# A parallel-branch decoder layer on one core: the work behind each z pair dealt out one step per product, a pair's last product one place later, and SSD groups at equal distances

## The chip, the cores and the metric

The kernel runs on one core of one Trainium2 chip. The metric is device time in microseconds (us) of one execution. The engines are TensorE (PE; its weight loads are listed as PEld), VectorE (DVE), ScalarE (ACT), GpSimd (POOL) and SyncE (SP). Each takes its instructions in the order in which the program lists them. SP issues most loads, POOL most stores, and ACT a few loads.

## The reference

One layer with x of 1024 tokens by 1024 channels in float32:

```
xn   = rms_norm(x)
proj = xn @ w_in                       # za, zb, zc, xbc, dt, gates: 10256 columns
ya   = gmlp(za)                        # chunked spatial gating, 8 groups
yb   = gelu(gate) * rg_lru(conv(xb))   # 8 heads of 128 channels
y    = ssd(conv(xbc), dt)              # 4 groups of 256 channels, chunks of 128 tokens
yc   = group_rms_norm(y * silu(zc)) * norm_g        # each group of 256 channels by itself
h    = x + (sum over a,b,c of sigmoid(g_k) * (y_k @ w_branch_k)) @ w_out
out  = rms_norm(h + relu(rms_norm(h) @ w_up)^2 @ w_down)
```

The line that this case turns on is yc: `z` is one of the projections, and after it is known there is a tanh (for the silu), two multiplications, a square, a sum over 256 channels, a reciprocal root and one more multiplication.

## The kernel before, in words

All large products are made of float32 operands split in a high and a low part (`split`, L128 to L133: ACT writes the high part, DVE subtracts it for the low part), with three matmuls for each block (high by high, high by low, low by high).

The program has five stages, in this order of the span: the normalised input and the first v blocks; the *first stage proper* (units of one weight column of 128, by `one_unit`, L558: 48 matmuls of 128x512 each and then a `post` function on the result); the *pair stage*; the merge of the three branches and w_out; and the MLP.

**Units (L1025 to L1045).** Four SSD groups, each with four units (b, c, x0, x1), stand in the queue with LRU heads between them: after group 0 the heads 0 and 1, after group 1 the heads 2 and 3, after group 2 the head 4 alone, after group 3 the heads 5, 6 and 7 (6 and 7 have a second unit each for the gate). Eight gMLP units follow. When the last unit of a group is posted, a generator (`ssd_stages`, L644) is put on the list `pending`. `step()` (L539) takes every pending generator one `yield` further, and runs once per unit. An SSD group's generator has eight such parts: broadcast rows of the decay are loaded, then transposes, products and the decay (`s1_`), the states (`s2_`), the outputs (`s3_`), and the same for the other half of the tokens. `s1_` and `s3_` take PSUM tiles `aux`, of which there are four in all: `s3_` takes four of them (two each for `yo` and `yi`). In this stage a scheduler sets the final order of instructions on each engine.

**Pairs (L901 to L1013).** The gates of the three branches (kind "t"), the z projection of the SSD branch ("z") and six of the eight LRU gate columns ("g") are not units but pairs of columns, and each pair is a 256-wide product done by a seven-product scheme on halves (`seventh`, L473: 12 matmuls of 128x512). The products are called p1, p2, p5, p6, p3, p7, p4 in their order. p1, p6, p7 and p4 add into one PSUM tile, `b1` (of the pool `gps`, four tiles); p5 and p3 into `b2` (an `aux` tile); p2 uses a `gps` tile of its own. So a product that adds into a tile waits until the engine that read it last has done so:

- after p1 ACT copies b1 (L971); p6 adds into b1 next
- after p2 DVE adds its tile to the copy (L976)
- after p5 ACT copies b2 (L982); p3 adds into b2 next
- after p6 ACT copies b1 (L988); p7 adds into b1 next
- after p3 DVE adds (L992), after p7 DVE adds (L996); p4 adds into b1 next
- after p4 ACT copies or gates (L915, L917)

There are 19 pairs, in the order t z t g t, t z t g t, t z t g t, z t t t. The loop that runs them is L1269 to L1311, with the order of the program kept as written. During a pair the weights of the next one are prepared: `cast1`, `cast12`, `cast34`, `cast22` are splits (one ACT and one DVE instruction each), `sums1` and `sums2` are four DVE additions (L502 to L507). p4 of the pair before (`prev.p4()`) stands behind p1 of the present pair. `step()` runs after each product, seven times per pair.

**Behind a z pair.** When a half (512 tokens) of a z pair is complete, `post_z` (L943 to L965) becomes pending: half 1 after p7, half 0 after p4. Its parts before the change, one per step: (A and B) tanh on ACT, two DVE multiplications of 128x1024, square on ACT; (C) a DVE addition of 128x512 (L950); an empty step; then all of (E to I): a matmul with a matrix of ones (L954), a root on ACT (L956, with a table load before it), a reciprocal on DVE (L957), four short DVE instructions (L958 to L961), two DVE multiplications (L964) and the store of the result on POOL's queue (L965). `post_g` (L933) does the like for a g pair in two parts: square, a DVE instruction and tanh; then two DVE multiplications and the store. The tiles `x` that they use come from a pool of four (`actx`).

Of the kernel before, what the change touches and what calls it, by code (L numbers as in the profile page):

```python
# [36 lines left out]
def trunk_kernel(ctx: ExitStack, tc: tile.TileContext, x, norm_mix_g, w_in, b_gate, gmlp_ln_g, gmlp_ln_b,  # L37
# [30 lines left out]
    def nm(s):  # L68
        uid[0] += 1
        return f"{s}_{uid[0]}"  # L70
# [7 lines left out]
    def aux():  # L78
        return auxp.tile([P, HF], F32, tag="aux", name=nm("aux"))
# [459 lines left out]
    def step():  # L539
        for g_ in list(pending):  # L540
            try:
                next(g_)
            except StopIteration:
                pending.remove(g_)
# [79 lines left out]
    def ssd_units(g):  # L624
        S = {}

        def xbc(key, ct):
            def post(ps):
                c = act()
                conv(c, ps, [scw[:, j * 16 + ct:j * 16 + ct + 1] for j in range(4)], vh[:, SCB + ct:SCB + ct + 1])  # L630
                t = act()
                actv(t, c, AF.Tanh)
                stt(out=c, in0=t, scalar=1.0, in1=c, op0=ALU.add, op1=ALU.mult)
                S[key] = c
                if key == "x1":
                    later(ssd_stages(g, S))
            unit_in(C_XBC + ct * P, post)

        xbc("b", 8 + g)
        xbc("c", 12 + g)  # L640
        xbc("x0", 2 * g)
        xbc("x1", 2 * g + 1)
# [109 lines left out]
    def lru_units(h):  # L752
# [60 lines left out]
        if h >= PLAIN:  # L813
            unit_in(C_GATE + h * P, post_g)
# [83 lines left out]
    def actx():  # L898
        return actx_pool[0].tile(list(two), F32, tag="actx", name=nm("x"))

    class Pair:  # L901
# [31 lines left out]
        def post_g(self, half):  # L933
            o, y, t = self.o[half], self.y[half], actx()
            actv(t, o, AF.Square)
            stt(out=t, in0=t, scalar=1.0 / GELU_C, in1=o, op0=ALU.add, op1=ALU.mult)
            actv(t, t, AF.Tanh, scale=GELU_S * GELU_C)
            yield
            stt(out=o, in0=t, scalar=1.0, in1=o, op0=ALU.add, op1=ALU.mult)
            tt(out=o, in0=o, in1=y, op=ALU.mult)  # L940
            nc.gpsimd.dma_start(out=self.part(yd["b"], half), in_=o)

        def post_z(self, half):  # L943
            o, y, t = self.o[half], self.y[half], actx()
            actv(t, o, AF.Tanh, scale=0.5)
            stt(out=o, in0=t, scalar=1.0, in1=o, op0=ALU.add, op1=ALU.mult)
            tt(out=o, in0=o, in1=y, op=ALU.mult)
            actv(t, o, AF.Square)
            yield
            tt(out=t[:, 0], in0=t[:, 0], in1=t[:, 1], op=ALU.add)  # L950
            yield
            yield
            vs = aux()
            mm(vs, ones, t[:, 0], start=True, stop=True)  # L954
            r, q = y[:, 0], y[:, 1]
            actv(r, vs, AF.Sqrt, scale=1.0 / 256, bias=eps4)  # L956
            nc.vector.reciprocal(out=r, in_=r)  # L957
            tt(out=q, in0=r, in1=r, op=ALU.mult)  # L958
            stt(out=q, in0=vs, scalar=256 * 4.0 * EPS, in1=q, op0=ALU.add, op1=ALU.mult)
            ts(out=q, in0=q, scalar1=-0.5 / 256, scalar2=1.5, op0=ALU.mult, op1=ALU.add)  # L960
            tt(out=r, in0=r, in1=q, op=ALU.mult)  # L961
            for b in range(2):
                col = SNG + self.e + b
                stt(out=o[:, b], in0=o[:, b], scalar=va[:, col:col + 1], in1=r, op0=ALU.mult, op1=ALU.mult)  # L964
            nc.gpsimd.dma_start(out=self.part(yd["c"], half), in_=o)  # L965
# [56 lines left out]
        yield  # L1022
        z.w.cast12()

    for r, heads in enumerate(((0, 1), (2, 3), (4,), (5, 6, 7))):  # L1025
        ssd_units(r)
        for h in heads:
            lru_units(h)
# [52 lines left out]
    def w_load(b, name, new, key=None):  # L1081
        L[b, key or name] = [new(two) for _ in range(2)]
        for h, t in enumerate(L[b, key or name]):
            nc.sync.dma_start(out=t, in_=w_view(b, name, h))
# [7 lines left out]
    def y_first(b, new):  # L1092
        R[b, "first"] = [new(two, F32R) for _ in range(2)]
        for h, t in enumerate(R[b, "first"]):
            nc.sync.dma_start(out=t.bitcast(F32), in_=y_view(b, "B21", h))
# [10 lines left out]
    def sums_load(b):  # L1106
        w_load(b, "A21", w4, "S")
        for h in range(2):
            add_into(L[b, "S"][h], w_view(b, "A22", h))
# [10 lines left out]
    def make(b, i, s):  # L1120

        side, h = (s // 2) ^ (i == 3), s % 2
        new = op_new(b, i, side)
        pr = OP.setdefault((b, i), ([], []))[side]
        if side == 0:
            src = L[b, ("A12", "A11", "S", "A12", "S", "A21", "A22")[i]][h]
            hi, lo = new(two, F32R), new(two, F32R)
            split(hi, lo, src)
            if i == 2:
                actv(src, src, AF.Copy, scale=-1.0)  # L1130
                add_into(src, L[b, "A11"][h])
                for k in range(2 * h):
                    add_into(L[b, "A12"][k], L[b, "S"][k])
            elif i == 4:
                t = L[b, "A21"][h]
                tt(out=t, in0=L[b, "A11"][h], in1=t, op=sub)
        elif i == 0:
            lo = R[b, "first"][h]
            hi = new(two, F32R)
            split(hi, lo, lo.bitcast(F32))  # L1140
        else:
            hi, lo = new(two, F32R), new(two, F32R)
            split(hi, lo, R[b, ("", "B11", "B11", "B22", "B11", "B12", "B21")[i]][h])
            r = lambda name: R[b, name][h]
            if i == 1:
                tt(out=r("B11"), in0=r("B12"), in1=r("B11"), op=sub)
            elif i == 3:
                tt(out=r("B11"), in0=r("B11"), in1=r("B22"), op=sub)
                tt(out=r("B12"), in0=r("B22"), in1=r("B12"), op=sub)
            elif i == 4:  # L1150
                tt(out=r("B21"), in0=r("B21"), in1=r("B11"), op=ALU.add)
        pr.append((hi, lo))
# [115 lines left out]
    z, prev = cur.pop(), None  # L1268
    with tc.manual_schedule():  # L1269
        z.w.cast22()  # L1270
        while z:
            nxt = Pair(*pairs.pop(0)) if pairs else None
            z.p1()
            z.w.cast34()
            step()
            if prev:
                prev.p4()
                step()
            z.p2()
            if nxt:  # L1280
                nxt.w.cast1()
            else:
                w_load(0, "A12", r4)
                y_first(0, act)
                w_load(0, "A11", w4)
            step()
            z.p5()
            if nxt:
                nxt.w.sums1()
            else:  # L1290
                make(0, 0, 2)
            step()
            z.p6()
            if nxt:
                nxt.w.sums2()
                nxt.w.cast12()
            else:
                sums_load(0)
                make(0, 0, 3)
            step()  # L1300
            z.p3()
            if nxt:
                nxt.w.cast22()
            else:
                make(0, 0, 0)
            step()
            z.p7()
            if not nxt:
                make(0, 0, 1)
            step()  # L1310
            prev, z = z, nxt  # L1311
# [312 lines left out]
    with tc.manual_schedule():  # L1624
# [75 lines left out]
        for s in range(2, NS):  # L1700
            last = s == NS - 1
            nxt = weights.get(s + 1)
            z = Super(s, weights[s])
# [140 lines left out]
```

## Time and profile before

| | |
|---|---|
| time, median of 3 runs | 2037.72 us (2036.15 to 2042.98) |
| the profiled execution: time, span | 2035.92 us, 2033.9 us |
| PE busy, share of the span | 1927.3 us, 95% |
| DVE, ACT, POOL busy | 1414.1, 1005.9, 293.6 us |
| mean granted clock of TensorE | 0.976 |
| the stage of the units | about 140 to 617 us of the span |
| the pair stage | about 617 to 1060 us of the span |
| idle of PE before the ones product (L954) | 35.1 us in 8 waits |

A row of a timeline has its start in us from the span's start, its duration in us, engine, line, operation, output tile and input tiles, shape, how many instructions are merged in it, and in brackets the idle time of the engine before it and what ended it. Matmuls are pipelined, so the start of the next row tells when a group is through, not the duration. "x24" with 12 matmuls per product is two products.

### The profile page before, as it was taken

The page shows a single profiled execution, that of the slowest core. Times are in us where ns is not written, and L with a number is a line of the kernel's source. Part 1 is how long each engine was busy: PE and PEld are TensorE (multiplying, and loading weights), DVE is VectorE, ACT ScalarE, POOL GpSimd, SP SyncE. Part 2 cuts the span into 40 slices and gives each one's busy share as a digit, 9 for nine tenths or more (in the row PEclk, how much of TensorE's full clock was granted, in tenths as well). Part 3 has the DMA queues.
Part 4 walks back from the last instruction along what each step waited for, and adds up shares of the span by engine and source line. Part 5 has one row for each costly group of instructions (what it writes and reads, how often), then busy time and mean ns, then how long its engine had stood idle before and what let it go on. Part 6 is the DMA issues. An engine that isn't in the chain of part 4 may idle for free.

```text
span 2033.9 us, 23784 instructions
## 1 busy us (share of the span) xinstructions
PE 1927.3 (95%) x8928; PEld 1597.7 (79%) x8928; DVE 1414.1 (70%) x2000; ACT 1005.9 (49%) x1455; POOL 293.6 (14%) x392
## 2 busy tenths in 40 slices
PE   8999999999999797989799999999899999999996
PEld 7998878778887585867688888787688887888885
DVE  5585868767768657566748789536756557787787
ACT  6435857558533444444445445246555555253243
POOL 4111313314332000000010101000111111000000
PEclk9999999999999899999899999999999999999998
DMA  4246555664754342423269798521444438634532
GB/s 156 71 144 139 116 128 136 129 138 108 173 146 135 97 131 84 139 91 122 73 221 306 197 295 202 176 93 54 164 139 157 161 133 299 217 130 143 185 107 92
DMA packets 211015, 301.25 MB, mean 148 GB/s; under 512 B 13028, under 2 KB 125876, under 8 KB 210900
## 3 DMA queue, kind: packets, MB, share of 16 engines
q1 hardware_dynamic: 167348, 158.54, 25.5%
q0 software_dynamic: 34544, 119.69, 21.9%
q10 hardware_dynamic: 9008, 21.51, 3.0%
q8 instruction: 70, 1.15, 0.2%
q14 instruction: 45, 0.37, 0.1%
HBM read 195.75 MB, written 74.58 MB: 133 GB/s over the span
## 4 chain that ended last, share of the span: by engine, by line
PE 59%; DVE 15%; ACT 7%; issue 4%; DMA 3%; POOL 0%; SPq 0%; ACTq 0%; DVEq 0%; POOLq 0%
PE aux L478 39%; PE ps L555 8%; PE gps L478 7%; PE aux L1366 2%; DMA a<-acs_d 1%; DVE x L957 1%; ACT wt L132 1%; DVE a L133 1%; ACT a L1415 1%; DVE a L578 1%; PE aux L789 1%; DMA lr<-in_lru_w_i_dram 1%; DVE rsq_q L111 1%; ACT L956 1%; DVE wt L133 1%
## 5 line engine op out<-in xcount | busy, mean ns | idle before, releaser
L555 PE MATMUL ps<-xn,wh 128*128 128x512 f32 x1088 | 296.1, 393 | 0.0
L478 PE MATMUL aux<-b,b 128*128 128x512 f32 x1152 | 263.7, 389 | 0.0
L478 PEld LDWEIGHTS aux<-b,b 128*128 128x128 f32 x1152 | 216.1, 188 | 45.1 <-DVE b L133 0.3
L555 PEld LDWEIGHTS ps<-xn,wh 128*128 128x128 f32 x1088 | 203.6, 189 | 42.1 <-issue 0.5
L478 PE MATMUL aux<-a,b 128*128 128x512 f32 x960 | 219.4, 389 | 0.0
L478 PEld LDWEIGHTS aux<-a,b 128*128 128x128 f32 x960 | 180.2, 188 | 37.4
L555 PE MATMUL ps<-xn,wl 128*128 128x512 f32 x544 | 168.4, 390 | 0.0
L478 PE MATMUL gps<-xn,wt 128*128 128x512 f32 x684 | 163.2, 392 | 2.4 <-DVE a L238 2.4
L478 PE MATMUL aux<-b,wt 128*128 128x512 f32 x672 | 156.9, 389 | 0.0
L478 PEld LDWEIGHTS gps<-xn,wt 128*128 128x128 f32 x684 | 129.4, 189 | 29.9 <-issue 2.8
L478 PEld LDWEIGHTS aux<-b,wt 128*128 128x128 f32 x672 | 126.1, 188 | 26.2
L133 DVE TENSOR_TENSOR wt<-a,wt 128x1024 fp32r<-128x1024 f32 x66 | 80.9, 1225 | 83.8 <-ACT wt L132 83.8
L132 ACT ACTIVATE b<-wt 128x1024 fp32r<-128x1024 f32 x88 | 90.7, 1052 | 84.8 <-DMA wt<-u_d 66.9
L555 PEld LDWEIGHTS ps<-xn,wl 128*128 128x128 f32 x544 | 102.4, 188 | 21.6
L133 DVE TENSOR_TENSOR b<-wt,b 128x1024 fp32r<-128x1024 f32 x88 | 107.1, 1218 | 15.5 <-ACT b L132 15.5
L1596 DVE TENSOR_TENSOR a<-aux,a 128x512 f32<-128x512 f32 x112 | 77.0, 688 | 50.4 <-PE aux L478 50.4
L133 DVE TENSOR_TENSOR a<-a,a 128x1024 fp32r<-128x1024 f32 (+1 forms) x68 | 66.6, 986 | 38.9 <-ACT a L132 38.8
L132 ACT ACTIVATE wt<-a 128x1024 fp32r<-128x1024 f32 x66 | 69.6, 1055 | 44.8 <-DVE a L506 44.5
L478 PE MATMUL aux<-a,wt 128*128 128x512 f32 x336 | 78.7, 390 | 3.3 <-ACT a L1473 3.3
L132 ACT ACTIVATE a<-a 128x1024 fp32r<-128x1024 f32 (+1 forms) x68 | 55.9, 837 | 50.5 <-DVE a L1548 45.2
L133 DVE TENSOR_TENSOR wt<-rt,wt 128x1024 fp32r<-128x1024 f32 x35 | 42.9, 1225 | 53.3 <-ACT wt L132 53.3
L478 PEld LDWEIGHTS aux<-a,wt 128*128 128x128 f32 x336 | 62.9, 188 | 17.2 <-ACT a L1473 4.2
(349 smaller groups left out, 3576.9 us busy)
## 6 DMA issues: line engine op xcount, KB each, us to landing
wt<-u_d SPq DMA_DIRECT2D x54, 512.0 KB
u_d<-a POOLq DMA_DIRECT2D x48, 512.0 KB, 5.4
raw<-in_w_in_dram SPq DMA_DIRECT2D x34, 512.0 KB
wl<-raw POOLq DMA_DIRECT2D x34, 512.0 KB, 5.2
g_d<-a POOLq DMA_DIRECT2D x24, 512.0 KB, 3.8
a<-g_d ACTq DMA_DIRECT2D x24, 512.0 KB
rt<-in_w_in_dram SPq DMA_DIRECT2D x19, 512.0 KB
a<-in_w_in_dram SPq DMA_DIRECT2D x19, 512.0 KB
```

The costliest lines, as they stand in the source:

```text
L111: stt(out=q, in0=r, scalar=nh, in1=r, op0=ALU.mult, op1=ALU.mult)
L132: actv(dst_hi, src, AF.Copy)
L133: (eng or nc.vector).tensor_tensor(out=dst_lo, in0=src, in1=dst_hi.bitcast(F32), op=ALU.subtract)
L478: mm(ps, lhs[l][kk], rhs[r][kk], start=(new and n == 0), stop=(n == 11), skip_group_check=not new)
L555: mm(ps[:, hsl(h)], w[wi][:, k, :], a.rhs(ai, k, h), start=(n == 0), stop=(n == 3 * KD - 1))
L578: stt(out=dst[:, j:], in0=ps[:, :T - j], scalar=taps[3 - j], in1=dst[:, j:], op0=ALU.mult, op1=ALU.add)
L789: mm(ps, w[wi][:, q * P:(q + 1) * P], S["xs"][half][ai], start=(n == 0), stop=(n == 2))
L956: actv(r, vs, AF.Sqrt, scale=1.0 / 256, bias=eps4)
L957: nc.vector.reciprocal(out=r, in_=r)
L1366: mm(ps, M.tok(a, k, c), wo[nb][k][w], start=(k == 0 and a + w == 0), stop=(k == KD - 1 and a == 1))
L1415: actv(Nf[th, k // 2][:, k % 2, (c % 4) * P:(c % 4 + 1) * P], ps[:, i * P:(i + 1) * P], AF.Identity, scale=g2c[:, KD + k:KD + k + 1])
L1596: tt(out=h, in0=ps, in1=h, op=ALU.add)
```

## The change

Three things are changed.

1. `post_z` gets a `yield` between nearly all of its parts. They are now: A (tanh, first multiplication), B (second multiplication, square), C (sum of the two columns), an empty step, E (ones product, root), F (reciprocal), G (L958, L959), H (L960, L961), I (L964 and the store). For half 0 three empty steps stand ahead of A. `post_g` gets one more `yield`, between its two last multiplications.
2. In the pair loop `prev.p4()` moves behind `z.p2()`; there are still seven steps per pair, now after p1, p2, p4 of the pair before, p5, p6, p3 and p7.
3. The LRU heads between the SSD groups are (0, 1), (2, 3), (4, 5), (6, 7) in place of (0, 1), (2, 3), (4), (5, 6, 7).

Lines of the changed kernel from `post_g` on are numbered up to nine higher: the reciprocal is L963 there, the ones product L959.

```diff
             actv(t, t, AF.Tanh, scale=GELU_S * GELU_C)
             yield
             stt(out=o, in0=t, scalar=1.0, in1=o, op0=ALU.add, op1=ALU.mult)
+            yield
             tt(out=o, in0=o, in1=y, op=ALU.mult)
             nc.gpsimd.dma_start(out=self.part(yd["b"], half), in_=o)
 
         def post_z(self, half):
             o, y, t = self.o[half], self.y[half], actx()
+            if half == 0:
+                for _ in range(3):
+                    yield
             actv(t, o, AF.Tanh, scale=0.5)
             stt(out=o, in0=t, scalar=1.0, in1=o, op0=ALU.add, op1=ALU.mult)
+            yield
             tt(out=o, in0=o, in1=y, op=ALU.mult)
             actv(t, o, AF.Square)
             yield
...
             mm(vs, ones, t[:, 0], start=True, stop=True)
             r, q = y[:, 0], y[:, 1]
             actv(r, vs, AF.Sqrt, scale=1.0 / 256, bias=eps4)
+            yield
             nc.vector.reciprocal(out=r, in_=r)
+            yield
             tt(out=q, in0=r, in1=r, op=ALU.mult)
             stt(out=q, in0=vs, scalar=256 * 4.0 * EPS, in1=q, op0=ALU.add, op1=ALU.mult)
+            yield
             ts(out=q, in0=q, scalar1=-0.5 / 256, scalar2=1.5, op0=ALU.mult, op1=ALU.add)
             tt(out=r, in0=r, in1=q, op=ALU.mult)
+            yield
             for b in range(2):
...
-    for r, heads in enumerate(((0, 1), (2, 3), (4,), (5, 6, 7))):
+    for r, heads in enumerate(((0, 1), (2, 3), (4, 5), (6, 7))):
...
             z.p1()
             z.w.cast34()
             step()
+            z.p2()
             if prev:
+                step()
                 prev.p4()
-                step()
-            z.p2()
             if nxt:
                 nxt.w.cast1()
```

What that does to the order is shown at three places.

DVE in the pair behind the first z pair, before: from the low part of a weight split to the sum of half 0 (x_5753), on which the second ones product waits. `x_5655` belongs to half 1.

```order
L133 TENSOR_TENSOR wt_5773<-rt_5716,wt_5772 128x1024
L957 RECIPROCAL x_5655<-x_5655 128x512
L958 TENSOR_TENSOR x_5655<-x_5655 128x512
L959 SCALAR_TENSOR_TENSOR x_5655<-aux_5776,x_5655 128x512
L960 TENSOR_SCALAR x_5655<-x_5655 128x512
L961 TENSOR_TENSOR x_5655<-x_5655 128x512
L964 SCALAR_TENSOR_TENSOR a_5653<-a_5653,va,x_5655 128x512 x2
L950 TENSOR_TENSOR x_5753<-x_5753 128x512
```

The same place now (the reciprocal of half 1, L963, stands two rows ahead of the first of these; `a_5602` is half 0, `a_5653` half 1, `x_5771` the sum of half 0).

```order
L133 TENSOR_TENSOR a_5828<-a_5715,a_5828 128x512
L965 TENSOR_TENSOR x_5655<-x_5655 128x512
L966 SCALAR_TENSOR_TENSOR x_5655<-aux_5792,x_5655 128x512
L950 SCALAR_TENSOR_TENSOR a_5602<-x_5771,a_5602 128x1024
L1005 TENSOR_TENSOR a_5785<-gps_5718,a_5785 128x512
L968 TENSOR_SCALAR x_5655<-x_5655 128x512
L969 TENSOR_TENSOR x_5655<-x_5655 128x512
L952 TENSOR_TENSOR a_5602<-a_5602,x_5709 128x1024
L133 TENSOR_TENSOR wt_5875<-a_5789,wt_5874 128x1024
L973 SCALAR_TENSOR_TENSOR a_5653<-a_5653,va,x_5655 128x512 x2
L955 TENSOR_TENSOR x_5771<-x_5771 128x512
```

The sum of half 0 was right behind half 1's root; now half 0's two multiplications, an evacuation and a weight split stand between them, and the sum itself closes the list.

ACT behind a g pair (the second), before: from the copy of p1 to the copy of p5 (L982); L935 and L937 are the square and the tanh of the g pair's half 0.

```order
L971 ACTIVATE a_6693<-gps_6680 128x512
L132 ACTIVATE wt_6695<-a_6619 128x1024
L917 ACTIVATE a_6563<-gps_6550 128x512
L935 ACTIVATE x_6715<-a_6563 128x1024
L937 ACTIVATE x_6715<-x_6715 128x1024
L132 ACTIVATE wt_6733<-rt_6676 128x1024
L982 ACTIVATE a_6753<-aux_6740 128x512
```

And now:

```order
L980 ACTIVATE a_6693<-gps_6680 128x512
L132 ACTIVATE wt_6695<-a_6611 128x1024
L917 ACTIVATE a_6548<-gps_6535 128x512
L132 ACTIVATE wt_6729<-rt_6676 128x1024
L935 ACTIVATE x_6733<-a_6548 128x1024
L937 ACTIVATE x_6733<-x_6733 128x1024
L991 ACTIVATE a_6750<-aux_6737 128x512
```

The square and the tanh now stand right ahead of the copy of p5, with the weight split before them.

PE in the stage of the units, before: the end of `s3_` of group 2 (L727) and the transposes of `s1_` of group 3 (L669).

```order
L723 MATMUL aux_4080<-a_3139,h_3967 128x128 x2
L727 MATMUL aux_4081<-a_3767,h_3848 64x128 x4
L727 MATMUL aux_4081<-a_3770,h_3857 64x128 x4
L669 MATMUL aux_4104<-ident,a_3829 128x128
L669 MATMUL aux_4104<-ident,a_3952 128x128
```

And now, at the end of `s3_` of group 2:

```order
L723 MATMUL aux_4119<-a_3139,h_4025 128x128 x2
L727 MATMUL aux_4120<-a_3779,h_3906 64x128 x4
L727 MATMUL aux_4120<-a_3782,h_3915 64x128 x4
L555 MATMUL ps_4151<-xn_224,wh_3956 128x512
L555 MATMUL ps_4151<-xn_537,wh_3956 128x512
```

The 48 matmuls of a whole unit now stand between the two.

## The prediction

> **What bounds the kernel now.** I read the page first, then busy time by stage, then PE's waits in the pair stage, then the timeline around the longest of them.
>
> ```profile
> PE 1927.3 (95%) x8928; PEld 1597.7 (79%) x8928; DVE 1414.1 (70%) x2000; ACT 1005.9 (49%) x1455; POOL 293.6 (14%) x392
> ```
>
> PE bounds the whole. By stage (columns: stretch, length, then busy time of PE, PEld, DVE, ACT and POOL with the number of instructions, granted clock, share of DMA, GB/s):
>
> ```profile
> 140.00:617.00 477.00, 465.95 (x2409) 388.10 (x2408) 345.79 (x486) 288.19 (x418) 147.28 (x180) 0.99 0.59 135
> 617.00:1060.00 443.00, 392.66 (x1633) 313.44 (x1633) 286.22 (x323) 196.61 (x248) 37.71 (x44) 0.95 0.38 119
> ```
>
> The pair stage leaves PE idle for 50 of 443 us, and its clock is the lower one. What PE waits for there (total, times, longest), and what DVE waits for from 640 to 1056 us:
>
> ```profile
> PE aux L954 <- DVE x L950: 35.1, 8, 8.0
> PE gps L478 <- DVE a L996: 10.8, 7, 3.1
> ...
> DVE wt L133 <- ACT wt L132: 86.3, 53, 3.7
> ```
>
> PE's timeline around the first z pair, and the same two points of the last one:
>
> ```profile
> 657.12 5.60 PE L478 MATMUL gps<-xn,wt 128*128 128x512 f32 x24
> ...
> 668.93 1.10 PE L954 MATMUL aux<-x,ones 128*128 128x512 f32 x2 [0.77 <-DVE x L950]
> 669.46 3.33 PE L478 MATMUL aux<-h,wt 128*128 128x512 f32 x12
> ...
> 683.50 2.04 PE L954 MATMUL aux<-x,ones 128*128 128x512 f32 x2 [7.99 <-DVE x L950]
> 684.56 4.94 PE L478 MATMUL aux<-xn,wt 128*128 128x512 f32 x12
> ...
> 697.59 2.81 PE L478 MATMUL gps<-a,a 128*128 128x512 f32 x7 [2.62 <-DVE a L996]
> ...
> 702.02 2.89 PE L478 MATMUL gps<-xn,wt 128*128 128x512 f32 x12
> ...
> 977.08 5.60 PE L478 MATMUL gps<-xn,wt 128*128 128x512 f32 x24
> ...
> 1020.42 2.88 PE L478 MATMUL gps<-xn,wt 128*128 128x512 f32 x12
> ```
>
> From z's p7 (657.12) to the p2 of the second pair behind it (702.02) are ten products. An undisturbed product takes 2.72 us (1028.58 to 1031.30, in the next rows), so 27.2 of these 44.9 us are work, and a z pair costs 17.7 us on top; the last of the four costs 43.34 - 27.2 = 16.1. The mean, 16.9, times four is 67.6 us. It consists of the ones products themselves (0.53 us for the first, 668.93 to 669.46; 1.06 for the second, after which the clock is still low), waits of 0.8, 8.0 and some 2 us, and slowed products: the one behind the long wait shows 4.94 where 2.88 is usual, 2.1 us lost.
>
> Why 8.0: these are the engines that feed the second ones product.
>
> ```profile
> 669.95 1.23 DVE L947 TENSOR_TENSOR a<-a,x 128x1024 f32<-128x1024 f32 x1
> ...
> 671.27 1.06 ACT L948 ACTIVATE x<-a 128x1024 f32<-128x1024 f32 x1 [2.77 <-DVE a L947]
> 672.24 1.05 ACT L132 ACTIVATE wt<-rt 128x1024 fp32r<-128x1024 f32 x1
> ...
> 673.32 1.23 DVE L133 TENSOR_TENSOR wt<-rt,wt 128x1024 fp32r<-128x1024 f32 x1 [1.53 <-ACT wt L132]
> ...
> 675.32 3.35 DVE L957 RECIPROCAL x<-x 128x512 f32<-128x512 f32 x1 [0.77 <-ACT x L956]
> ...
> 678.70 0.69 DVE L958 TENSOR_TENSOR x<-x 128x512 f32<-128x512 f32 x1
> 679.43 0.69 DVE L959 SCALAR_TENSOR_TENSOR x<-aux,x 128x512 f32<-128x512 f32 x1
> 680.15 0.43 DVE L960 TENSOR_SCALAR x<-x 128x512 f32<-128x512 f32 x1
> 680.62 0.69 DVE L961 TENSOR_TENSOR x<-x 128x512 f32<-128x512 f32 x1
> 681.34 1.42 DVE L964 SCALAR_TENSOR_TENSOR a<-a,va,x 128x512 f32<-128x512 f32 x2
> 682.67 0.68 DVE L950 TENSOR_TENSOR x<-x 128x512 f32<-128x512 f32 x1
> ```
>
> Half 0's sum (L950) stands on DVE behind the whole root of half 1: 7.3 us without a gap from 675.32.
>
> **The change: behind a z pair.** The DVE work stays the same. One pair of any kind needs three full splits of 1.23, a short one of 0.68, and seven additions of 0.69: 9.2 us. A z pair adds, for each half, two of 1.23 and 0.68 + 3.35 + 0.69 + 0.69 + 0.43 + 0.69 + 1.42: 20.8 us for both. So the pair behind z had 30 us of DVE work for 19 us of PE work; spread over two pairs it is 39.2 for 38.1. It fits no better than just, and what counts is the order in it.
>
> *First ones product.* Its sum now stands behind p2, the product itself behind p5, two products later; 0.77 goes, 0.53 stays.
>
> *Second ones product.* Half 0's sum is now the last item in the step behind the next pair's p1, the ones product stands behind the p4 that follows. I count from the end of p6 in the pair behind z, where half 1's reciprocal is next on DVE, behind a weight split. What that split takes, from a pair without such work (1028.58 is the end of p6, 1031.30 that of p3):
>
> ```profile
> 1028.58 2.88 PE L478 MATMUL aux<-xn,wt 128*128 128x512 f32 x12
> 1028.78 0.60 ACT L988 ACTIVATE a<-gps 128x512 f32<-128x512 f32 x1 [1.51 <-PE gps L478]
> 1029.27 1.05 ACT L132 ACTIVATE wt<-a 128x1024 fp32r<-128x1024 f32 x1
> ...
> 1030.36 1.23 DVE L133 TENSOR_TENSOR wt<-a,wt 128x1024 fp32r<-128x1024 f32 x1 [2.35 <-ACT wt L132]
> 1031.30 5.60 PE L478 MATMUL gps<-xn,wt 128*128 128x512 f32 x24
> 1031.50 0.69 DVE L992 TENSOR_TENSOR a<-aux,a 128x512 f32<-128x512 f32 x1
> ...
> 1048.31 1.05 ACT L132 ACTIVATE a<-a 128x1024 fp32r<-128x1024 f32 x1
> ```
>
> - Copy, high part, low part: DVE is free at 1031.59, 3.0 us after p6.
> - Then on DVE, in the order shown for the changed kernel: 3.35, evacuation 0.69, short split 0.68, 0.69 + 0.69, half 0's first multiplication 1.23, evacuation 0.69, 0.43 + 0.69, half 0's second multiplication 1.23: 10.4. Neighbours that don't depend on each other overlap a little (681.34 to 682.67 is 1.33 for 1.42): 10.0.
> - Hand-over: DVE to ACT for the square, then a copy and a split on ACT, before DVE has work again. 671.18 to 673.32 shows square and split, 2.1; with the copy (0.5) 2.6.
> - On DVE: low part 1.23, half 1's last two 1.42, the sum 0.68: 3.3. To PE 0.15 (683.35 to 683.50).
>
> Sum 19.0 us. PE has p3, p7, p1, p2 and p4 meanwhile: 13.6. A wait of 5.4 us remains of the 8.0, and it moves to the second pair behind z.
>
> *p4 behind p2.* The evacuation of p7 (L996) now has 5.4 instead of 2.7 us before p4 needs it. It ends in the same count after 3.0 + 3.35 + 0.69 + 0.68 + 0.69 + 0.69 + 1.23 + 0.69 = 11.0, less overlap 10.7; PE reaches p4 after four products, 10.9. The wait of about 2 goes, with 0.2 us to spare; if that cover is missing it costs up to 0.5.
>
> *The clock.* Does a wait of 5.4 us still slow the next product? The nearest rows, and the wait in the stage of the units that comes up below:
>
> ```profile
> 439.66 0.66 PE L669 MATMUL aux<-ident,a 128*128 128x128 f32 x4
> 444.84 1.11 PE L669 MATMUL aux<-ident,a 128*128 128x128 f32 x4 [4.52 <-DVE h L730]
> 445.60 2.05 PE L555 MATMUL ps<-xn,wh 128*128 128x512 f32 x4
> ...
> 449.60 0.62 PE L555 MATMUL ps<-xn,wl 128*128 128x512 f32 x2
> ...
> 622.42 4.58 PE L478 MATMUL gps<-xn,wt 128*128 128x512 f32 x12 [2.38 <-DVE a L238]
> ...
> 737.89 3.06 PE L478 MATMUL gps<-a,a 128*128 128x512 f32 x12 [0.34 <-DVE a L996]
> ...
> 924.62 3.02 PE L478 MATMUL gps<-a,a 128*128 128x512 f32 x12 [1.86 <-DVE a L996]
> ```
>
> Behind 4.52 us, ten matmuls took 4.0 us (445.60 to 449.60) instead of 2.3, and the four small ones before them 0.5 more: 2.2 lost. Behind 2.38 us a product took 1.7 more, behind 1.86 us only 0.1. So I take 2.1 us, and 1.06 for the ones product. [...]
>
> A z pair then costs 0.53 + 5.4 + 1.06 + 2.1 = 9.1 us instead of 16.9: 4 x 7.8 = 31.2 us gained.
>
> **Behind a g pair.** `post_g` has one more step, and half 0's square and tanh now come one product closer to p5, right ahead of the copy of p5 on ACT, on which p3 depends. The tanh waits for a DVE instruction that stands behind the low parts of two splits, the two last multiplications of half 1 and an evacuation: with itself five of 1.23 and one of 0.69, 6.8 us, 6.4 with the overlaps. By a count like the one above, the first of them starts 1.1 us before p4 ends (ACT has the tanh of half 1, a copy and a split ahead of it). Then tanh 1.06, copy 0.5, hand-over 0.2: 7.1 us after p4's end, where p5 and p6 take 5.4. So p3 comes some 1.6 us late. Before, 0.34 us were waited and 0.18 lost behind it (737.89: 3.06 for 2.88). Bounds: 0.3 as now, 3 if the DVE backlog from z is not yet worked off. At 1.7 instead of 0.5, three times: 3.6 us lost.
>
> **SSD groups.** The wait of 4.52 us at 444.84 is `s1_` of group 3 wanting an `aux` tile that `s3_` of group 2 still holds, five units after group 2 in place of six. In the new order a unit stands between. 4.5 + 2.2 go; a wait like that behind 1.86 us may come in the moved part, some 1.4: 5.3 gained, between 0 and 6.7.
>
> **The rest.** The last z store is later by eight products and is read back for the merge, where ACT needs it at 1048.31; it is done by about the p2 of the last pair, near 1040. 8 us hide store and load, up to 3 if not. The weight loads on SP and the gate stores on POOL wait for earlier steps than those moved. Table loads are as many as before.
>
> Sum, against the profiled execution (2035.92 us, 1.8 below the median of the runs): 2035.9 - 31.2 + 3.6 - 5.3 = 2003.0. I give 2003 for the median too.
>
> **The rivals.**
>
> - *A wait of 5.4 us leaves the clock alone.* The rows: 924.62 speaks for it, 444.84 and 622.42 against. 4 x (2.1 + 0.53) = 10.5 less: 1992.5. Chance 0.20. [...]
> - *All is hidden.* If DVE were let at half 0's sum as soon as ACT's square is done, 5.4 would shrink to about 0, and the g waits too. The order speaks against it. 4 x 8.6 + 3.6 = 38 less: 1965. Chance 0.08.
> - *The long wait only moves.* If the 8.0 us stay whole and p4 loses its 0.2 us of cover, a z pair costs 13.5: 4 x 3.4 = 13.6 gained, 2035.9 - 13.6 + 3.6 - 5.3 = 2020.6. For it: the same DVE work stands ahead of the same sum. Chance 0.14.
> - *DVE becomes the bound: slower.* The three pairs behind z, with the g pair's 7.4 us, hold 3 x 9.2 + 20.8 + 7.4 = 55.8 us of DVE work for 58.7 of PE. Before, they took 57.1 + 16.9 + 0.5 = 74.5. DVE's waits for ACT's half of a split are 1.63 us each, 14.7 in nine splits. If each step's hand-over doubled them (29.4), the three pairs would take 85.2 us: 4 x 10.7 - 5.3, 2073. It decides from 21.6 us of DVE waits in three pairs. Against it: the work is the same, with fewer items per step. Chance 0.03.
>
> **How the numbers follow.** The forecast has 0.55. About 0.3% (6.1 us) is what a measurement can tell from no change. All cases but the last are faster by more: 0.95, with 0.02 for no difference and 0.03 for slower. Low end: the clock rival, less 3.6 if the g waits don't grow, less 3: 1986. High end: waits 1 us longer (4), nothing gained on the groups (5.3), g waits at 3 (3.9), 2 at the merge: 2018. That leaves out the hidden case, the slow one and the upper part of the third.
>
> **What would show it.** PE's wait before the first ones product gone; before the second one, now in the second pair behind z, some 5 us instead of 8, with a slow product behind it; no wait for the p7 evacuation; 1 to 2 us before p3 behind g pairs, released by ACT's copy; no wait of 4.5 us near 440. I am wrong if the second wait is under 3 or over 7 us, or if DVE's waits for ACT grow by more than 20 us.

## The result, and the profile after

| | before | after |
|---|---|---|
| time, median | 2039.15 us (4 runs, 2036.15 to 2042.98) | 2010.54 us (4 runs, 2009.01 to 2012.24) |
| the profiled execution: time, span | 2035.92 us, 2033.9 us | 2009.9 us, 2007.9 us |
| mean granted clock of TensorE | 0.976 | 0.982 |

The ratio of the medians is 0.9859, 95% interval 0.9839 to 0.9879: faster by 28.6 us, where 2003.0 us, 32.9 less than the profiled execution of before, was forecast. The profiled executions differ by 26.0 us, and the rest of this section says where these lie.

First the busy times by stage, with the stretches cut at the same instructions in both kernels: from the first s3_ of group 2 to the first pair product, and from there to the merge's first product. Columns: stretch, length, then busy time of PE, PEld, DVE, ACT, POOL, granted clock, DMA share, GB/s. Before:

```profile
394.67:617.07 222.40, 217.24 (x1162) 182.96 (x1160) 159.33 (x204) 122.61 (x174) 78.95 (x83) 0.98 0.58 138
...
617.07:1056.86 439.79, 389.45 (x1619) 310.74 (x1618) 284.87 (x322) 193.84 (x244) 36.97 (x43) 0.95 0.38 118
```

After:

```profile
394.13:621.18 227.05, 219.27 (x1161) 183.53 (x1160) 159.51 (x204) 126.13 (x176) 81.37 (x88) 0.98 0.56 136
...
621.18:1031.64 410.46, 384.00 (x1620) 309.19 (x1618) 278.37 (x321) 193.29 (x244) 35.90 (x43) 0.97 0.40 125
```

The pair stage is 29.3 us shorter (forecast: 31.2 - 3.6 = 27.6). The end of the stage of the units, with all but the same number of instructions (1161 matmuls for 1162), is 4.65 us longer (forecast: 5.3 shorter). What lies ahead is 0.5 us shorter, what lies behind (977.0 us before, 976.3 after) 0.8: 29.3 - 4.65 + 0.5 + 0.8 = 26.0.

What PE waits for in the pair stage after (total, times, longest; the rows that are new or changed):

```profile
PE aux L959 <- DVE x L955: 19.3, 4, 4.8
PE aux L478 <- ACT a L991: 3.0, 3, 1.0
```

The eight waits before ones products are four, the seven before p4 (10.8 us) are gone, and three short ones before p3 are new. PE's timeline from the first z pair's p7 on:

```profile
660.94 8.32 PE L478 MATMUL gps<-xn,wt 128*128 128x512 f32 x36
...
674.55 1.02 PE L959 MATMUL aux<-x,ones 128*128 128x512 f32 x2
...
678.14 2.88 PE L478 MATMUL aux<-xn,wt 128*128 128x512 f32 x12
...
696.71 2.04 PE L959 MATMUL aux<-x,ones 128*128 128x512 f32 x2 [4.81 <-DVE x L955]
697.77 5.37 PE L478 MATMUL aux<-h,wt 128*128 128x512 f32 x12
702.98 2.90 PE L478 MATMUL gps<-h,wt 128*128 128x512 f32 x12
...
959.54 8.32 PE L478 MATMUL gps<-xn,wt 128*128 128x512 f32 x36
...
996.04 4.76 PE L478 MATMUL aux<-h,wt 128*128 128x512 f32 x12
1000.64 2.88 PE L478 MATMUL gps<-h,wt 128*128 128x512 f32 x12
```

From z's p7 (660.94) to the p6 of the second pair behind it (702.98) are twelve products, 32.6 us at 2.72; they take 42.0. The first z pair now costs 9.4 us, the two that follow 9.4 and 9.3, the last (959.54 to 1000.64) 8.5, where 17.7 and 16.1 were lost in the first and the last before and 9.1 was forecast. The product behind the wait takes 697.77 to 702.98, 5.2 us, 2.5 more than 2.72. Not all of that is the clock: behind the first ones product, which did not wait, the product takes 3.1 us too (675.00 to 678.14), so 2.1 are lost to the lower clock, as forecast. The granted clock (the third number from the end) is 0.50 there, and 1.00 from 660 to 690 us:

```profile
695.40:702.10 6.70, 5.39 (x11) 3.61 (x12) 6.69 (x7) 1.49 (x2) 1.42 (x2) 0.50 0.67 197
```

DVE in front of that ones product, from the reciprocal of half 1 to the sum of half 0:

```profile
681.06 3.35 DVE L963 RECIPROCAL x<-x 128x512 f32<-128x512 f32 x1
...
693.41 1.23 DVE L133 TENSOR_TENSOR wt<-a,wt 128x1024 fp32r<-128x1024 f32 x1 [2.62 <-ACT wt L132]
694.56 1.41 DVE L973 SCALAR_TENSOR_TENSOR a<-a,va,x 128x512 f32<-128x512 f32 x2
695.88 0.68 DVE L955 TENSOR_TENSOR x<-x 128x512 f32<-128x512 f32 x1
```

p6 of this pair ends at 678.14, the ones product starts at 696.71: 18.6 us, where the count had 19.0.

In the stage of the units (140 to 612 us), what PE waits for after:

```profile
PE aux L789 <- ACT a L677: 4.2, 1, 4.2
PE aux L789 <- DVE h L714: 3.3, 2, 2.0
PE aux L703 <- DVE h L673: 2.1, 2, 1.2
PE aux L703 <- ACT a L576: 2.1, 1, 2.1
PE aux L789 <- DVE h L729: 1.9, 3, 0.6
```

The wait of 4.52 us at 444.84 is gone, as forecast; together these are 13.6 us, where PE's waits in this stage before sum to 10.9. The longest is new: L789, the gate products of an LRU head, wants an `aux` tile that the transposes of an `s1_` (L676) hold until ACT has copied it (L677). ACT and PE around it:

```profile
500.60 1.28 ACT L690 ACTIVATE a<-a,acs 128x128 f32<-128x128 f32 x4 [1.39 <-DMA a<-acs_d]
...
503.71 0.60 PE L676 MATMUL aux<-ident,a 128*128 128x128 f32 x4
504.15 2.43 ACT L690 ACTIVATE a<-a,acs 128x128 f32<-128x128 f32 x8
506.62 1.06 ACT L691 ACTIVATE a<-a 128x1024 f32<-128x1024 f32 x1
...
508.48 1.05 ACT L526 ACTIVATE wh<-raw 128x1024 fp32r<-128x1024 f32 x1
509.43 0.59 ACT L677 ACTIVATE a<-aux 128x512 f32<-128x512 f32 x1
510.07 0.96 PE L789 MATMUL aux<-h,lw 128*128 128x512 f32 x3 [4.18 <-ACT a L677]
```

PE is through with the transposes at 504.3; the copy stands in ACT's queue behind decays (L690, L691; one of them waited 1.39 us for its DMA) and work of the unit, the last of it a weight split (L526), and starts 5.1 us later. In the stretch as a whole PE's idle time is 7.8 us (227.05 - 219.27) where it was 5.2, and its busy time 2.0 us more for the same matmuls; why the matmuls took longer at the same mean granted clock, 0.98, the rows don't show.

### The profile page after: what moved, and what is told of

It is laid out like the page before. It is cut to its first block, busy times and chain, and to the rows that moved or that the text cites. A ratio compares the mean times of both kernels' runs of the same rounds, so it can differ in the third digit from the quotient of the medians.

```text
span 2007.9 us, 23777 instructions
## 1 busy us (share of the span) xinstructions
PE 1923.5 (96%) x8928; PEld 1596.5 (80%) x8928; DVE 1406.7 (70%) x2000; ACT 1005.3 (50%) x1455; POOL 293.1 (15%) x392
## 4 chain that ended last, share of the span: by engine, by line
PE 55%; DVE 11%; ACT 6%; issue 4%; DMA 2%; POOL 0%; ACTq 0%; SPq 0%; DVEq 0%; POOLq 0%
PE aux L478 39%; PE gps L478 8%; PE ps L555 4%; PE aux L1375 2%; DMA wt<-in_w_branch_c_dram 1%; ACT wt L132 1%; DVE wt L133 1%; DMA a<-acs_d 1%; DVE a L133 1%; ACT a L1424 1%; DVE rsq_q L111 1%; PE aux L959 1%; DVE b L133 1%; ACT a L132 1%; PE aux L836 0%
```

## The experiments

The theory after this comparison: the steps behind z do what was counted, and the regrouping of the heads took one wait away and made others. The rivals: the groups are worth their 5.3 us and the pair stage fell short; or p4's new place carries part of the gain that was put down to the steps. Each run below was timed beside runs of the kernel before (medians 2037.81 to 2039.52 us), in four groups on four chips: pairs, heads, steps and p4 only; one and two steps later, heads apart and the changed kernel again; the tanh later and all; and the last two. Differences between runs of different groups below are between medians, and can be off by the 1.7 us by which the medians of before differ.

| run | median, us | ratio to before, 95% interval |
|---|---|---|
| pairs only | 2006.35 | 0.9845 (0.9827 to 0.9864) |
| heads only | 2038.76 | 1.0001 (0.9992 to 1.001) |
| steps only | 2007.72 | 0.984 (0.9824 to 0.9857) |
| p4 only | 2021.82 | 0.9918 (0.9905 to 0.9932) |
| ones product one step later | 2006.22 | 0.9842 (0.9828 to 0.9855) |
| two steps later | 2006.97 | 0.9845 (0.9832 to 0.9859) |
| heads apart | 2003.66 | 0.9828 (0.9814 to 0.9841) |
| the changed kernel again | 2010.15 | 0.986 (0.9847 to 0.9874) |
| two steps and the tanh later | 1984.27 | 0.9727 (0.9713 to 0.974) |
| all | 1979.71 | 0.9705 (0.9691 to 0.9718) |
| all, p4 ahead | 2002.49 | 0.9818 (0.9805 to 0.9831) |
| all, heads as changed | 1984.80 | 0.9733 (0.972 to 0.9747) |

### Pairs only, heads only

The changed kernel with the heads as before, and the kernel before with the heads as changed:

```diff
-    for r, heads in enumerate(((0, 1), (2, 3), (4, 5), (6, 7))):
+    for r, heads in enumerate(((0, 1), (2, 3), (4,), (5, 6, 7))):
```

> The changed kernel with the LRU heads as before, (0, 1), (2, 3), (4,), (5, 6, 7); the pair loop and the two post functions as changed. Theory A (the regrouping of the heads made the stage of the units longer: 227.05 us from the first s3_ of group 2 to the first pair product against 222.40 before, because the wait of 4.52 us went and waits of 4.18, 2.04 and 0.93 us came): that stretch is back at 222.4, the first pair product starts near 617, the pair stage is as in the changed kernel (410.5 us), and the time is 2010.5 - 4.6 = 2006. Rival B (the regrouping is worth the 5.3 us that were forecast for it, and the gain falls short elsewhere): 2010.5 + 5.3 = 2016.

> The kernel before with the LRU heads as changed, (0, 1), (2, 3), (4, 5), (6, 7), and nothing else. Theory A: slower by 4.6 us, 2039.2 + 4.6 = 2044, with the wait of 4.2 us of L789 for L677 near 510 us and no wait of 4.5 us near 440. Rival B: faster by 5.3 us, 2034.

Pairs only took 2006.35 us, as theory A had it, 4 us below the changed kernel (2010.54, and 2010.15 when timed again), though the intervals of the ratios overlap. From the first s3_ of group 2 to the first pair product it takes 221.9 us (394.14 to 616.03), where the two profiles of the changed kernel have 227.05 and 227.6, and its waits in the stage of the units are 11.0 us in all, with one of 4.4 where before has 4.52. Heads only has the waits of the changed kernel there:

```profile
PE aux L789 <- DVE h L714: 4.6, 3, 2.0
PE aux L789 <- ACT a L677: 4.1, 1, 4.1
```

Its profiled span, 2036.9 us, is 3.0 longer than that of before. Its median is not: the ratio is 1.0001 and leaves room for 1.6 us gained or 2.0 lost. So rival B (5.3 gained) has fallen. Theory A's 4.6 us lost are seen in part in this profile (3.0) and, as some 4, beside the changed pairs; in the times of heads only they are not there, and 2044 was wrong. Part of this may be that the profiled execution of before lies 2.8 us under the median of its 17 runs beside this one; no run settles it.

### Steps only, p4 only

The yields of `post_z` and `post_g` without the move of p4, and the move of p4 without the yields; both with the heads as before. The edit of the second against the kernel before:

```diff
-            z.p2()
             if prev:
-                step()
                 prev.p4()
+                step()
+            z.p2()
```

> The kernel before with the new yields in post_z and post_g alone; the product p4 of the pair before stays ahead of p2, the heads are as before. The forecast's account: the waits before the ones products fall to one of about 5 us per z pair, but p4 waits again for the DVE evacuation of p7, some 1.5 us in seven pairs, 10.8 us in all: 2006 + 10.8 = 2017. Rival (p4's place is worth nothing, since what p4 waits is taken off the ones wait behind it): 2006.

> The kernel before with p4 of the pair before behind p2 and nothing else; post_z, post_g and the heads as before. The forecast's account: the waits of p4 for L996 (10.8 us in seven) go, those before the ones products (35.1 in eight) stay: 2039.2 - 10.8 = 2028. Rival (the queue on DVE is what counts, and what p4 no longer waits the second ones product waits more): 2039.

Alone, the steps give 31 us and p4's place 17; together 32. The gains don't add, and on top of the steps p4's place is worth 1.4 us, less than these intervals can tell from nothing. The profile of steps only shows why. Its waits in the pair stage, and the timeline behind the first z pair:

```profile
PE gps L478 <- DVE a L1005: 20.8, 11, 3.3
...
686.43 5.49 PE L478 MATMUL gps<-a,a 128*128 128x512 f32 x12 [3.33 <-DVE a L1005]
691.71 1.46 PE L959 MATMUL aux<-x,ones 128*128 128x512 f32 x2
```

The ones product waits for nothing: p4, one product ahead of it, waits 3.33 us for p7's evacuation, which stands in the same DVE queue, and the product behind the wait is slowed as well: p4 itself takes 5.3 us (686.43 to 691.71) where 2.72 is usual. Here the wait earlier in the order covers the later one. In p4 only it is the other way round: p4's waits shrink to 2.6 us, and what waits is p3, for ACT's copy, nearly as long as the second ones product did.

```profile
PE aux L478 <- ACT a L982: 31.4, 7, 7.8
PE gps L478 <- DVE a L996: 2.6, 4, 0.7
```

So the long wait stayed, as expected for p4 only (2028). The gain was larger, 17 for 10.8. In the profiled executions it is 13.9 (2035.92 to 2022.06): the pair stage is 11.6 shorter (439.79 to 428.19 us, 616.92 to 1045.11), close to what was counted, and what lies behind it 2.1. The other 3 are that the profiled execution of before lies below its median; no run settles more.

### The ones product later

```diff
             tt(out=t[:, 0], in0=t[:, 0], in1=t[:, 1], op=ALU.add)
             yield
             yield
+            if half == 0:
+                for _ in range(1):
+                    yield
```

This is added to pairs only; the second kernel has `range(2)` there.

> The kernel of the run with the pair edits alone (heads as before), with one empty step more for half 0 between its sum and its ones product, so that the ones product stands one product later. Theory (the 19.0 us from the end of p6 to the sum are fixed by DVE's and ACT's queues, and PE has one product more to put over them): the wait of 4.8 us becomes 4.8 - 2.7 = 2.1 us; four z pairs save 10.8 us, 2006.4 - 10.8 = 1995.6. Whether a product behind a wait of 2.1 us is slowed is open: rows of the stage of the units have it slowed behind 2.04 and 2.38 us and not behind 1.86; if it is not slowed, 4 x 2.6 us more, 1985. Rival (the wait only moves, since half 0's later steps move with it and another product waits for DVE in its place): 2006.

> As the run with one empty step more, but with two. Theory: 4.8 - 5.4 is below 0, so the ones product waits no longer, nothing behind it is slowed, and it costs 0.5 instead of 1.06 us: 4 x (4.8 + 2.6 + 0.5) = 31.6 us less than with the pair edits alone, 2006.4 - 31.6 = 1974.8. Rival: the backlog of DVE comes out at another place, p4 or the p3 behind the g pair, and half of the gain or more is lost there: 1990 to 2006.

No change in time, 2006.22 and 2006.97: the rival (for two steps at the upper end of its 1990 to 2006). With one step the wait shrinks exactly as counted, from 4.8 to 2.1 us, and the p3 behind the g pair, which waited 1.0 us, waits 4.4, with a slowed product behind it:

```profile
691.54 1.10 PE L962 MATMUL aux<-x,ones 128*128 128x512 f32 x2 [2.10 <-DVE x L955]
692.07 4.89 PE L478 MATMUL gps<-h,wt 128*128 128x512 f32 x12
696.80 2.90 PE L478 MATMUL aux<-xn,wt 128*128 128x512 f32 x12
...
720.44 4.42 PE L478 MATMUL aux<-xn,wt 128*128 128x512 f32 x12 [4.42 <-ACT a L994]
```

In the kernel with two no ones product waits, and p3 waits 6.39 us behind all three g pairs. DVE, ACT and PE there:

```profile
713.02 1.40 DVE L976 SCALAR_TENSOR_TENSOR a<-a,va,x 128x512 f32<-128x512 f32 x2
714.34 1.22 DVE L941 TENSOR_TENSOR a<-a,x 128x1024 f32<-128x1024 f32 x1
715.47 1.22 DVE L133 TENSOR_TENSOR wt<-rt,wt 128x1024 fp32r<-128x1024 f32 x1
716.61 1.22 DVE L936 SCALAR_TENSOR_TENSOR x<-x,a 128x1024 f32<-128x1024 f32 x1
...
717.86 1.06 ACT L937 ACTIVATE x<-x 128x1024 f32<-128x1024 f32 x1 [4.21 <-DVE x L936]
718.82 0.58 ACT L994 ACTIVATE a<-aux 128x512 f32<-128x512 f32 x1
...
719.46 5.43 PE L478 MATMUL aux<-xn,wt 128*128 128x512 f32 x12 [6.39 <-ACT a L994]
```

p3 needs ACT's copy of p5 (L994). In ACT's queue the tanh of the g pair's half 0 (L937) stands ahead of it and waits 4.21 us for DVE's L936, which stands behind z's last multiplications, the g pair's half 1 and a split. The copy itself depends on none of these. In the last pair PE also waits 3.2 and 1.3 us for splits of operands of the merge; ACT waits 5.95 us there for a load of `yc`, the result of the last z pair.

### The tanh later

On two steps later, one more yield in `post_g`:

```diff
             stt(out=t, in0=t, scalar=1.0 / GELU_C, in1=o, op0=ALU.add, op1=ALU.mult)
+            yield
             actv(t, t, AF.Tanh, scale=GELU_S * GELU_C)
```

> The kernel with the pair edits and two empty steps more for half 0 of a z pair (heads as before), and in post_g one yield more, between the DVE instruction on the square and the tanh, so that ACT copies p5 for p3 before it waits for that DVE instruction. Theory (in the run with two empty steps the wait of 6.39 us came to p3 behind each g pair because ACT's queue held the copy of p5 behind the tanh of post_g, and the tanh waited for DVE; no engine was full): the three waits of 6.39 us and the three slowed products behind them, 2.5 us each, go: 2007.0 - 26.7 = 1980. Rival (DVE has too much work in the pairs behind z, and the wait comes out at the next product that needs DVE, the p4 or p7 behind): 2000 to 2007.

1984.27 us where 1980 was expected, 22.7 less than without this line, and the intervals are far apart. The waits before p3 are gone; of the 26.7 us expected 4 are not there, and three waits of 1.3 us for ACT's copy of p6, behind the tanh at its new place, are:

```profile
719.69 8.46 PE L478 MATMUL gps<-xn,wt 128*128 128x512 f32 x36 [1.31 <-ACT a L1001]
```

DVE does the same work as before (278.6 us busy in the pair stage, 619.34 to 1007 us, where it was 284.9), so it was not the bound: what bound the pairs was the order of two queues. The line was tried only on top of the two steps, not on pairs only.

### Heads apart, and all edits together

Six units between all SSD groups again, but with other heads, so that no gated head is posted in the step of group 3's second `s1_`; first on pairs only:

```diff
-    for r, heads in enumerate(((0, 1), (2, 3), (4,), (5, 6, 7))):
+    for r, heads in enumerate(((0, 1), (2, 3), (6,), (4, 7, 5))):
```

> The pair edits with the LRU heads (0, 1), (2, 3), (6,), (4, 7, 5): six units between all SSD groups, as in the change, but no head with its gate posted in the step of s1_ of group 3's second half. Theory (it was the meeting of head 7 and that s1_, which holds its tile until ACT has copied it behind the decays, that cost the 4.2 us wait, and equal distances do take away the wait of 4.5): neither wait is there, the stretch from the first s3_ of group 2 to the first pair product is 222.4 - 5.3 = 217 us, and the time 2006.4 - 5.3 = 2001. Rival (equal distances only move the wait to the next head that meets a group's stage): 2006 to 2010.

> The changed kernel once more, on the same chip as the three beside it, to set the price of the heads: theory (heads as changed cost 4 us): 2010.5, 4 us above the pair edits alone; rival (as the run with the heads alone says, no price that can be measured): 2006.4.

The waits of 4.5 and of 4.2 us are both gone, and those of the stage sum to 9.7 us (11.0 in pairs only, 13.9 in the changed kernel again). So equal distances do take away the one, and it was the meeting that made the other. 2003.66 us is 6.5 less than the changed kernel again, with intervals that don't overlap. But the gain of 5.3 us over the heads as before did not come: the stretch is 220.5 us (395.92 to 616.40) where 217 was expected and pairs only has 221.9, the first pair product starts no earlier (616.40 and 616.03), and that the time is less than that of pairs only (2006.35) the intervals don't tell.

The run with all edits adds these heads to the tanh later, and for half 0 of the last z pair makes one step of G, H and I:

```diff
+            short = half == 0 and self.e == 6
+            if not short:
+                yield
...
+            if not short:
+                yield
```

> As the run with the tanh one step later, with the heads (0, 1), (2, 3), (6,), (4, 7, 5), and, for half 0 of the last z pair alone, the steps G, H and I as one, so that its store is issued two products earlier. Theory: 2.7 us for the heads (2003.7 against 2006.4 in the earlier runs), and the waits of 3.2 and 1.3 us in the last pair for the store of the last z, read back, are gone: 1980 - 2.7 - 4.5 = 1973. Rival (as for the run before; and the heads are worth nothing where the pairs wait less): 1980 or more.

1979.71 us, the fastest here: 2.95% less than before (2.8 to 3.1%), and 31 us below the changed kernel. 1973 was expected; the 4.6 us to the run with the tanh later are in place of 7, and the intervals of these two overlap, so what these edits are worth on top of the tanh the times don't tell (1979.71 is the rival's 1980). The wait of 3.2 us in the last pair (3.6 in the tanh run) is gone, that of 1.3 stayed. Most of the pair stage now runs at full clock:

```profile
617.00:1000.00 383.00, 373.63 (x1617) 303.64 (x1616) 276.85 (x320) 194.19 (x246) 37.01 (x44) 1.00 0.43 135
```

Two single edits taken back from it, p4's place and the heads:

> The kernel of the last run (later ones product and tanh, heads apart, the last z pair's short end), with p4 of the pair before ahead of p2 again, as in the kernel before. Theory (the later place of p4 covers DVE's evacuation of p7, which stands in the same queue as the work behind z; with the steps alone p4 waited 20.8 us in eleven): the wait in front of p4 is there again, 3.3 and 1.5 us behind a z pair and some 0.5 elsewhere, with a product slowed by 2.6 us behind the longest: 20.8 + 4 x 2.6 = 31 us more, 2011. Rival (p4's place is worth as little here as on top of the steps alone, 1.4 us): 1981.

> The kernel of the run with all edits, with the heads as changed, (0, 1), (2, 3), (4, 5), (6, 7), in place of (0, 1), (2, 3), (6,), (4, 7, 5). Theory (the meeting of head 7 with s1_ of group 3's second half costs what the pairs-only and the apart runs differ from the changed kernel): the wait of 4.2 us of L789 for L677 is back, 1979.7 + 6.5 = 1986. Rival (the price of the heads changes with the rest, as it was nothing on the kernel before): 1980.

With p4 ahead of p2 the time is 2002.49, 22.8 us more (31 expected): the waits before p4 are back.

```profile
PE gps L478 <- DVE a L1012: 20.2, 8, 3.7
```

So p4's place, worth nothing measurable beside the wait for the ones product, is worth 22.8 us once that wait is gone. With the heads as changed it is 1984.80, 5.1 us more than with the heads apart (6.5 expected; the intervals lie just beside each other), with the wait for L677 back:

```profile
510.36 1.03 PE L789 MATMUL aux<-h,lw 128*128 128x512 f32 x3 [4.11 <-ACT a L677]
```

## Why the prediction was right, and where it was off

- **Behind z: right, with its mechanism.** First ones wait gone, second one 4.8 us (5.4 forecast) at the place named, 18.6 us from the end of p6 to the ones product (19.0), a slowed product behind it in all four cases, 9.1 us per z pair on average (9.1). The reading that let this come out was the order of DVE's queue with durations of before put to each row. That the average agrees to the tenth is partly luck: the wait came out smaller, and the first ones product costs more than the 0.53 us put down for it, since the product behind it takes 3.1 us in place of 2.72 (675.00 to 678.14), and took 3.2 before the change.
- **The clock: right.** By the rival that a wait of 5.4 us leaves the clock alone, the four products would have taken about 3.1 us, as behind a ones product that does not wait; they took 5.2, 5.2, 5.1 and 4.6, and the granted clock behind the first wait is 0.50.
- **The third rival was added up wrong.** "A z pair costs 13.5" is not the sum of its terms: 0.53 + 8.0 + 1.06 + 2.1 and the 0.5 for p4 are 12.2, which would have been 2015 and inside the range. A wait of 4.8 us has ruled it out either way.
- **p4 behind p2: right that no wait for p7's evacuation stays.** What the prediction did not say is that on top of the steps this is no gain that can be measured: the same DVE backlog would have been waited for once, at p4 in place of the ones product (steps only).
- **g pairs: right in kind, too large.** p3 waits 1.0 us for ACT's copy (1.6 forecast) and loses 0.15 behind it, so three cost 1.9 us more than before in place of 3.6:

```profile
725.92 3.03 PE L478 MATMUL aux<-xn,wt 128*128 128x512 f32 x12 [1.00 <-ACT a L991]
728.78 3.56 PE L478 MATMUL gps<-xn,wt 128*128 128x512 f32 x15
```

- **SSD groups: the step that failed.** "5.3 gained, between 0 and 6.7." The old wait went, but the stretch grew by 4.65 us in the profiled executions: 5.3 + 4.65 = 10 us of error, which the better pair stage (1.7), and 1.3 in the stages around it, reduced to 6.9 (2009.9 against 2003.0). That the heads are the cause, the runs with other heads show: the stretch is some 5 us shorter in pairs only, and with the heads apart the time is 6.5 us less (all: 5.1). (An SSD group's generator is taken on in seven parts, not eight: the rows of the second half are loaded in the step of the first `s3_`. So with five units between two groups the last `s3_` of one meets the first `s1_` of the next in one step, and with six they stand in steps of their own.) The prediction asked what the heads had left behind and not what they would meet: head 7, by the order of the units, has its gate products in the step of the second `s1_` of group 3, and they wait for an `aux` tile until ACT has copied it. A moved unit brings its own tiles to other tenants of the pool, and the bounds, 0 to 6.7, should have reached below nothing.
- **DVE as the bound: rightly small.** DVE's waits for ACT's half of a split grew, from 86.3 us before (640 to 1056 us) to 105.1 after (640 to 1031 us):

```profile
DVE wt L133 <- ACT wt L132: 105.1, 46, 3.7
```

That is 18.8 us more, close to the 20 that were to count against the forecast, and the pair stage still came out 1.7 us shorter than forecast: this was slack. That sum was a poor sign to watch.

## What to carry to other kernels

Here DVE's backlog made several consumers late, and only the first of them showed it: moving that one gave the wait to the next, and the gains of separate moves did not add (31 and 17 us alone, 32 together). Follow such a backlog through all queues, and look for an instruction that waits at the head of a queue while one that needs nothing stands behind it: here a tanh that waited 4.21 us ahead of a copy, and one line that put it behind gave 23 us on top of an edit of the visible wait that had given nothing by itself. And when work is moved into a shared pool of tiles, ask what it meets there, not only what it leaves: here a wait of 4.52 us went and one of 4.18 us came.

## What the runs showed of the hardware

How long PE may wait before the next product is slowed. An undisturbed product takes 2.72 us, one behind a ones product that did not wait 3.1. Waits of 0.65, 1.0, 1.3 and 1.46 us left at most 0.2 us behind them, but for two in the last pair that had one of 3.2 or 3.56 us two matmuls ahead: there (two steps later, and the tanh later) the next product took 4.78 and 4.42 us. Behind the waits of 2.1 us before the ones product (one step later) the four products took 4.73, 4.28, 4.74 and 3.14 us: three were slowed, the fourth was not. The granted clock around the first and the fourth:

```profile
692.00:697.00 5.00, 5.00 (x15) 3.78 (x14) 3.63 (x5) 0.69 (x1) 0.51 (x1) 0.66 0.88 264
992.00:999.00 7.00, 4.90 (x21) 3.42 (x20) 6.70 (x10) 4.50 (x7) 1.42 (x2) 1.00 0.41 152
```

A wait of 2.20 us in the kernel before (p4 at 1017.55) also left the product behind it at 2.87 us. Behind 3.33 us (steps only) the four products took 5.29, 4.34, 4.45 and 5.29 us, and behind 6.39 (two steps later) 5.26, 5.14 and 5.06. So around 2.1 us it went either way, from 2.38 us on every wait that the rows of the pair stages show was followed by slowed products, and the loss, up to 2.6 us in these rows, did not grow with the wait. What decides between equal waits of 2.1 us the rows don't show. In the row at 691.54 the slowing begins only after the ones product, which took 0.53 us, as the first one of the kernel before did (668.93 to 669.46) at a granted clock of 1.00.
